# Where and when the first weights of an MLP are fetched and split, in a two-layer encoder

## The chip, the cores and the metric

The kernel runs on one core of one Trainium2 chip. The metric is the device time of one execution in microseconds (us), the median of several runs. The profile is a single execution taken by the hardware profiler.

## The reference

The program is a bidirectional encoder over 256 tokens with 1024 channels, of two layers, all in float32. Each layer has two sub-layers and each adds its result to the residual stream `h`:

```python
for layer in range(DEPTH):
    h = h + _token_mixer(_rmsnorm(h, norm1[layer]), ...)
    h = h + _conv_ffn(_rmsnorm(h, norm2[layer]), ...)
return _rmsnorm(h, norm_f)
```

The token mixer projects the normed tokens into a pooling branch, into queries, keys and values of 12 heads in three groups, and into two gates. Its end is what matters here:

```python
merged = jax.nn.sigmoid(g_pool) * (pool_out @ w_a) + jax.nn.sigmoid(g_attn) * (attn_out @ w_b)
return merged @ w_o
```

The MLP (`_conv_ffn`) multiplies the normed tokens by `w_up` (1024 x 5632), runs a width-3 convolution over tokens on the first half of the result, applies GELU, multiplies by the second half and then by `w_down` (2816 x 1024).

## The kernel before, in words

**Two-part numbers.** TensorE multiplies in a rounded float32 format. To keep float32 accuracy, each operand is split into a rounded high part and the low rest, and three products are summed: high x high, high x low and low x high. So every weight that arrives from memory is split before its use: ScalarE (ACT) casts the raw data to the high part (`wh`, line 197), and VectorE (DVE) subtracts it from the raw data to get the low part (`wl`, line 198).

**The stream of weights.** The class `Weights` holds one list of loads (1 MB each, 128 partitions x 2048 numbers, issued by SyncE, SP, at line 134) and one list of pieces, two for each load, in the order of use. A load goes to one of three rotating raw buffers (`RAW`), unless it has a `tag`: then it goes to the place of that name in a pool of large tiles, once the tile that had the place before is no longer read. A split piece goes to one of five rotating pairs `wh`, `wl` (`BUFS`), unless it has a `slot`: then it goes to a named large place as well. `get` hands out the next piece and has the pieces up to three further on split (`LOOK`); a piece with a slot may be split a little further ahead, since it takes none of the five pairs. Each split in turn asks for the loads up to two behind its own.

**Where an instruction stands in its queue.** Each engine works through its own queue in order. A scheduler puts the instructions there when the program is built. Two calls hold some of them back: `queue_behind(insts, n, first)` makes the splits of pieces `first` to `first + n - 1` stand behind the instructions `insts` in the queues of ACT and DVE, and `loads_behind` makes a load stand behind a given DMA in SP's queue.

**The stages around the change**, in each layer:
1. Scores of the attention heads. The last matmuls that read the keys of groups two and three (`kk`, place `k1`, line 998, named `k` in the trace) belong to the last head. They lie between the matmuls of `pool_out @ w_a`, which are line 643, as are all products that give rows of tokens.
2. The gates' stage: the pool gate in two halves of 512 channels (four loads of `w_in`), then for each half of the channels the attention gate (two loads of `w_in`) and `attn_out @ w_b` (one load).
3. The turn, once for each half: DVE multiplies gate and product (lines 1134, 1137), transposes 32 x 32 blocks (line 664), SP writes the result to memory (one DMA, `turned`, line 671) and reads it back by channels (four DMAs, `merged`, line 674), and ACT and DVE split it (lines 682, 683) into `m2`.
4. `residual_mm` with `w_o` (lines 561 to 563; eight pieces, of which the last four are held). The sum for the tokens is kept in four PSUM banks: token half 0 and 1, channels 0 to 511 and 512 to 1023. With the held pieces these are finished one after the other; the last one in two parts of 256 channels. As each is finished, `Norm.add` adds it to `h` on DVE (line 421) and sums its squares on ACT (line 423, `junk`). GpSimd (POOL) adds the two partial sums (line 432) and takes the power -1/2 (line 435). DVE scales four blocks of 256 channels (line 448, `xn`), PE transposes them to channels (line 457, `xt_ps`), and ACT and DVE split them (lines 460, 461) into `x2`, in the trace `x`.
5. The MLP's beginning (`begin_mlp`): the first 512 columns of `w_up`, in two loads, that is four pieces. The first three have slots: `v1` (the place of the values), `ybig` (of the product with `w_a`) and `at2` (of the attention's result); in the trace they are `v`, `ybig` and `at`. The fourth takes an ordinary pair `wh`, `wl`. PE's matmuls with these pieces are line 643 again, into `v_ps`.

The order of the four pieces and their loads is set at the end of the second turn (`n == 1`): the three loads from the MLP's first on stand behind the turn's last read (`there`), and the four pieces stand behind the split of that turn (`last`). The five pieces ahead of them, of `w_o`, stand behind the transposed blocks of the turn (`turned`).

Of the kernel before, what the change touches and what calls it, by code (L numbers as in the profile page):

```python
# [226 lines left out]
def encoder(ctx, tc, x, w_in, w_pool, pool_scale, w_a, w_b, w_o, norm1, norm2, w_up, conv_w,  # L227
# [11 lines left out]
    W = Weights(tc, wpool, big)  # L239

    def cols(w, c0):

        src = w[:, c0 : c0 + 256].rearrange("(k p) c -> p k c", p=P)
        return W.add(
            src, (8, 256), [((lambda t, j=j: t[:, :, j * P : (j + 1) * P]), (8, P)) for j in (0, 1)]
        )

    def rows(w, r0, n=2, c0=0, width=1024, tag=None, pieces=2):

        src = w[r0 : r0 + n * P, c0 : c0 + width].rearrange("(k p) c -> p k c", p=P)  # L250
        h = n // pieces
        return W.add(
            src, (n, width), [((lambda t, j=j: t[:, j * h : (j + 1) * h, :]), (h, width)) for j in range(pieces)],
            tag,
        )

    first_up = []
    for l in range(DEPTH):
        for g in range(NG):
            c0 = C_V + g * 512  # L260
            slots = (("m2", 0, 2), ("m2", 1, 2), ("ybig",), ("at2",)) if g == 0 else ()
            for j in range(2):
                tag = "k1" if l == 0 and g == 1 and j == 0 else None
                W.use(rows(w_in[l], j * 512, 4, c0, 512, tag), slots[2 * j : 2 * j + 2])
        if l == 0:
            W.n_scaled = len(W.pieces)
        for c in range(3, -1, -1):
            W.use(cols(w_in[l], c * 256))
        for n, c in enumerate(PAIRS):
            pool = ([], [])  # L270
            if n == 1:
                pool = W.add(
                    w_pool[l].rearrange("g (k p) c -> p (g k) c", p=P), (8, 256),
                    [((lambda t, j=j: t[:, 4 * j : 4 * j + 4, :]), (4, 256)) for j in range(2)],
                )
                pool = (pool[:1], pool[1:])
            W.use(pool[0] + cols(w_in[l], C_Q + c * 256))
            W.use(pool[1] + cols(w_in[l], C_K + c * 256))
        for w, c0 in ((w_a[l], 0), (w_in[l], C_GP)):
            for c in (c0, c0 + 512):  # L280
                W.use(rows(w, 0, 4, c, 512) + rows(w, 512, 4, c, 512))
        for c in (0, 512):
            W.use(rows(w_in[l], 0, 4, C_GA + c, 512) + rows(w_in[l], 512, 4, C_GA + c, 512))
            W.use(rows(w_b[l], 0, 4, c, 512))
        for c in range(4):
            W.use(rows(w_o[l], c * 256))
        first_up.append((len(W.pieces), len(W.loads)))
        slots = (("v1",), ("ybig",), ("at2",))
        for j in range(2):
            W.use(rows(w_up[l], j * 512, 4, 0, 512), slots[2 * j : 2 * j + 2])  # L290
        for f in range(0, NF, 2):
            a = cols(w_up[l], f * P) if f >= ENTRY else []
            g = cols(w_up[l], DFF + f * P)
            W.use([a[0], g[0], a[1], g[1]] if a else g)
            if f >= LAG:
                W.use(rows(w_down[l], (f - LAG) * P))
        for f in range(NF - LAG, NF, 2):
            W.use(rows(w_down[l], f * P))
# [349 lines left out]
    def by_tokens(x2, n, at_once=1, then=None):  # L648

        ps = [mmp.tile([P, 512], F32, tag="mm", name="t_ps") for _ in range(2)]  # L650
        for i0 in range(0, n, at_once):
            held = [W.get() for _ in range(at_once)]
            for t in range(2):
                for i, piece in enumerate(held, i0):
                    v_sum(ps[t], x2, t, i, piece, n - 1)
            for i, _ in held:
                W.free(i)
            if then:
                then()
        return ps  # L660

    def turn_blocks(y, t, rows):

        return nc.vector.transpose(out=y[:, :, :, t, :].rearrange("p q c j -> p c q j"), in_=rows)

    def to_chunks(y, z, x2):

        d = dram.tile([P, 4, 256], F32, tag="turned", bufs=2, name="turned")  # L670
        nc.sync.dma_start(out=d, in_=y.rearrange("p q c t j -> p q (c t j)"))
        for q in range(4):
            src = d[:, q].rearrange("(a i) x -> i a x", a=4)
            there = nc.sync.dma_start(
                out=z[32 * q : 32 * q + 32].rearrange("p a c t j -> p a (c t j)"), in_=src
            )
        for c in range(0, 4, 2):
            cs = slice(c, c + 2)
            src = z[:, :, cs].rearrange("p a c t j -> p a (c t) j")
            hi, lo = (p[:, cs].rearrange("p c t (a j) -> p a (c t) j", a=4) for p in x2)  # L680
            last = (
                nc.scalar.copy(out=hi, in_=src),
                nc.vector.tensor_sub(out=lo, in0=src, in1=hi.bitcast(F32)),
            )
        return there, last
# [179 lines left out]
    for l in range(DEPTH):  # L865
# [245 lines left out]
        def gate():  # L1111
            th = big.tile([P, 2, 512], F32, tag="gates", name="gates")
            ps = by_tokens(x2, 4)
            for t in range(2):
                nc.scalar.activation(th[:, t], ps[t], AF.Tanh, scale=0.5)
            return th
# [11 lines left out]
        for n, cc in enumerate(HALVES):  # L1128
            th = gate()
            ps = by_tokens(at2, 2, 2)  # L1130
            y = big.tile([P, 4, 4, 2, 32], F32, tag=("q0", "k0")[n], name="turned")
            for t in range(2):
                with tc.issue_after(last[1].ins) if n else ExitStack():
                    nc.vector.scalar_tensor_tensor(
                        out=th[:, t], in0=th[:, t], scalar=1.0, in1=ps[t], op0=ALU.add, op1=ALU.mult
                    )
                    nc.vector.tensor_add(out=th[:, t], in0=th[:, t], in1=pa[:, t, cc])
                    turned = turn_blocks(y, t, th[:, t])
                last = (None, turned)
            ks = slice(4 * n, 4 * n + 4)  # L1140
            there, last = to_chunks(y, z[:, n], (mh[:, ks], ml[:, ks]))

            piece, load = first_up[l]
            if n == 0:
                W.queue_behind((turned,), 1)
                W.loads_behind.update({load - 2: there, load - 1: there})
                W.queue_behind(last, 5, piece - 5)
            else:
                W.queue_behind((turned,), 5, piece - 5)
                W.loads_behind.update({load: there, load + 1: there, load + 2: there})  # L1150
                W.queue_behind(last, 4, piece)

        x2 = two_parts("x", "x2")
        norm = Norm(to_channels(x2, acc, g2))
# [28 lines left out]
        def keep_entry(ps):  # L1183
            r = sm.tile([P, ENTRY * P], F32, tag="p", bufs=3, name="a_rows")
            nc.scalar.copy(out=r, in_=ps)
            return r
# [17 lines left out]
        last = keep_entry(ps)  # L1204
# [99 lines left out]
```

## Time and profile before

| | us |
|---|---|
| median of three runs | 875.97 |
| lowest and highest run | 874.54, 877.9 |
| the profiled execution | 875.6 |
| its span, from the first to the last instruction | 873.8 |

How to read it: PE is TensorE's matmuls, DVE VectorE, ACT ScalarE, POOL GpSimd, SP SyncE, whose work here is to issue DMAs. A line of the timeline has the start and the duration in us, the engine, the line of the kernel, the operation, what it writes and reads, and the number of instructions put together; in brackets stands how long the engine was idle just before, and whose work ended that. Matmuls overlap: a row's duration is longer than the distance to the next row's start. A line of the waits has who waited for whom, the total in us, how often, and the longest. The mean granted clock of TensorE was 0.999 of full speed.

### The profile page before, as it was taken

Reading aid. Unit: us, or ns where it says so; the run is one execution under the profiler, and the core shown is the slowest. Engines: PE = TensorE matmul, PEld = TensorE weight load, DVE = VectorE, ACT = ScalarE, POOL = GpSimd, SP = SyncE. Lnnn points to the kernel's source line nnn. Section 1 sums busy time; section 2 is a strip of 40 time slices with the busy share of each in tenths; the row PEclk is TensorE's granted clock in tenths of the full one; section 3 lists DMA queues with packets and bytes.
Section 4 is the critical chain, followed back from the end, with each engine's and each line's share of the span. In section 5 each row is a group of like instructions: output and inputs, shape, how many; then the busy total and the mean of one; then the engine's idle time right before and its main releaser. Section 6 shows DMA issues by size and latency. Waiting matters only on the chain.

```text
span 873.8 us, 12139 instructions
## 1 busy us (share of the span) xinstructions
PE 864.0 (99%) x4583; PEld 744.5 (85%) x4583; DVE 662.2 (76%) x1070; ACT 510.2 (58%) x847; POOL 32.5 (4%) x98
## 2 busy tenths in 40 slices
PE   9999999999999999999999999999999999999997
PEld 8888888888878888888888889988888788888886
DVE  7998786656769978878855987765567798887884
ACT  7756554544457766666545674544444587666663
POOL 1800000000010000000000000000000100000000
PEclk9999999999999999999999999999999999999999
DMA  9676545445765465475636564453566446546531
GB/s 338 234 243 208 180 151 180 141 155 194 242 213 193 154 231 193 154 234 191 240 122 218 168 219 166 147 169 124 193 237 239 172 152 232 192 166 220 193 144 49
DMA packets 116547, 165.86 MB, mean 190 GB/s; under 512 B 3640, under 2 KB 84224, under 8 KB 116488
## 3 DMA queue, kind: packets, MB, share of 16 engines
q1 hardware_dynamic: 116328, 164.81, 55.8%
q8 instruction: 36, 0.59, 0.3%
q10 hardware_dynamic: 160, 0.27, 0.1%
q14 instruction: 23, 0.19, 0.1%
HBM read 161.90 MB, written 3.17 MB: 189 GB/s over the span
## 4 chain that ended last, share of the span: by engine, by line
PE 95%; DMA 2%; DVE 1%; ACT 1%; issue 0%; SPq 0%; POOL 0%; POOLq 0%; ACTq 0%; DVEq 0%
PE proj_ps L519 46%; PE t_ps L643 16%; PE v_ps L643 6%; PE res_ps L563 5%; PE res_ps L561 5%; PE res_ps L562 5%; PE v_ps L857 2%; PE v_ps L764 1%; PE pool_ps L519 1%; PE pt_ps L1027 1%; PE o_ps L1048 1%; PE s_ps L998 1%; DMA raw<-in_w_up_dram 1%; PE xt_ps L457 1%; PE s_ps L993 1%; PE o_ps L1044 1%
## 5 line engine op out<-in xcount | busy, mean ns | idle before, releaser
L198 DVE TENSOR_TENSOR wl<-raw,wh 128x1024 fp32r<-128x1024 f32 x274 | 333.5, 1222 | 140.2 <-ACT wh L197 99.2
L197 ACT CAST wh<-raw 128x1024 fp32r<-128x1024 f32 x274 | 286.3, 1049 | 137.1 <-PE t_ps L643 63.5
L519 PE MATMUL proj_ps<-x,wh 128*128 128x512 f32 x1152 | 274.6, 390 | 0.0
L519 PEld LDWEIGHTS proj_ps<-x,wh 128*128 128x128 f32 x1152 | 213.1, 188 | 42.2
L519 PEld LDWEIGHTS proj_ps<-x,wl 128*128 128x128 f32 x1152 | 144.9, 191 | 3.6
L519 PE MATMUL proj_ps<-x,wl 128*128 128x256 f32 x1152 | 147.9, 283 | 0.0
L643 PE MATMUL t_ps<-wh,x 128*128 128x512 f32 x256 | 79.7, 390 | 0.0
L561 PE MATMUL res_ps<-wh,actq 128*128 128x512 f32 (+1 forms) x184 | 70.0, 380 | 0.0
L562 PE MATMUL res_ps<-wl,actq 128*128 128x512 f32 (+1 forms) x184 | 69.9, 380 | 0.0
L563 PE MATMUL res_ps<-wh,actk 128*128 128x512 f32 (+1 forms) x184 | 69.9, 380 | 0.0
L643 PEld LDWEIGHTS t_ps<-wh,x 128*128 128x128 f32 x256 | 48.1, 188 | 9.9
L643 PE MATMUL t_ps<-wl,x 128*128 128x512 f32 x128 | 49.8, 389 | 0.0
L643 PE MATMUL t_ps<-wh,po 128*128 128x512 f32 x128 | 42.7, 399 | 0.0
L562 PEld LDWEIGHTS res_ps<-wl,actq 128*128 128x128 f32 x184 | 34.6, 188 | 6.6
L561 PEld LDWEIGHTS res_ps<-wh,actq 128*128 128x128 f32 x184 | 34.6, 188 | 6.6
L563 PEld LDWEIGHTS res_ps<-wh,actk 128*128 128x128 f32 x184 | 34.6, 188 | 6.6
L1230 ACT ACTIVATE y<-y 128x256 f32<-128x256 f32 x44 | 18.1, 417 | 28.5 <-DVE y L1221 28.4
L430 POOL TENSOR_SCALAR ss<-ss 128x1 f32<-128x1 f32 x8 | 2.4, 302 | 802.0 <-ACT junk L423 802.0
L1217 ACT ACTIVATE y<-a,prm 128x256 f32<-128x256 f32 x36 | 21.6, 600 | 14.8 <-DVE a L556 14.8
L643 PEld LDWEIGHTS t_ps<-wl,x 128*128 128x128 f32 x128 | 24.0, 188 | 5.0
L643 PEld LDWEIGHTS t_ps<-wh,po 128*128 128x128 f32 x128 | 24.1, 188 | 4.7
L563 PE MATMUL res_ps<-wh,m 128*128 128x512 f32 (+1 forms) x72 | 26.5, 369 | 0.0
(209 smaller groups left out, 1168.9 us busy)
## 6 DMA issues: line engine op xcount, KB each, us to landing
raw<-in_w_in_dram SPq DMA_DIRECT2D x58, 1024.0 KB, 5.6
raw<-in_w_up_dram SPq DMA_DIRECT2D x44, 1024.0 KB, 5.7
raw<-in_w_down_dram SPq DMA_DIRECT2D x22, 1024.0 KB, 4.7
raw<-in_w_a_dram SPq DMA_DIRECT2D x8, 1024.0 KB, 4.9
raw<-in_w_o_dram SPq DMA_DIRECT2D x8, 1024.0 KB
raw<-in_w_b_dram SPq DMA_DIRECT2D x4, 1024.0 KB
raw<-in_w_pool_dram SPq DMA_DIRECT2D x2, 1024.0 KB
turned<-turned SPq DMA_DIRECT2D x4, 512.0 KB
```

What stands on the lines that cost most here:

```text
L197: lambda: nc.scalar.copy(out=h, in_=src),
L198: lambda: nc.vector.tensor_sub(out=l, in0=src, in1=h.bitcast(F32)),
L457: nc.tensor.transpose(pt[:, k, :], xn[:, c0 : c0 + P], ident)
L519: nc.tensor.matmul(out, w(k), x, start=(steps is first and k == 0), stop=(steps is last and k == nk - 1), skip_group_check=turns["rest"],)
L561: nc.tensor.matmul(ps, ah, wh, start=first, stop=False, skip_group_check=on)
L562: nc.tensor.matmul(ps, ah, wl, start=False, stop=False, skip_group_check=on)
L563: nc.tensor.matmul(ps, al, wh, start=False, stop=last, skip_group_check=on)
L643: nc.tensor.matmul(ps, x2[:, 2 * n + j, part, t, :], w[:, j, :], start=(n + m == 0), stop=(n == last and m == 5),)
L764: return nc.tensor.matmul(ps[t], a[:, k, t, :], w[:, k % 2, :], start=first, stop=last)
L857: nc.tensor.matmul(ps[t], a[:, k, t, :], w[:, j, :], start=(k + m == 0), stop=(k == KD - 1 and m == 2),)
L1217: nc.scalar.activation(y, a, AF.Identity, bias=b, scale=w1)
L1230: nc.scalar.activation(y2, y, AF.Square, scale=float(np.sqrt(0.044715)))
```

## The change

The first load of the MLP's weights no longer takes a raw buffer. It goes to the place `k1` of the keys. It is taken out of the list of loads that stand behind the second turn's read, and the first of its two pieces is taken out of the pieces that stand behind the split of that turn. With nothing to hold it back, the load is issued when the keys are no longer read, and the piece is split as soon as `Weights` and the scheduler come to it, which is in the gates' stage. Its second piece, both pieces of the second load, and both later loads keep their places behind the turn. The computation is the same.

```diff
         slots = (("v1",), ("ybig",), ("at2",))
         for j in range(2):
-            W.use(rows(w_up[l], j * 512, 4, 0, 512), slots[2 * j : 2 * j + 2])
+            tag = None if j else "k1"
+            W.use(rows(w_up[l], j * 512, 4, 0, 512, tag), slots[2 * j : 2 * j + 2])
...
                 W.queue_behind((turned,), 5, piece - 5)
-                W.loads_behind.update({load: there, load + 1: there, load + 2: there})
-                W.queue_behind(last, 4, piece)
+                W.loads_behind.update({load + 1: there, load + 2: there})
+                W.queue_behind(last, 3, piece + 1)
```

## The prediction

> **What bounds the kernel now.** I read the page's busy times first, then what TensorE (PE) waited for, then the timeline of each engine around that wait.
>
> ```profile
> PE 864.0 (99%) x4583; PEld 744.5 (85%) x4583; DVE 662.2 (76%) x1070; ACT 510.2 (58%) x847; POOL 32.5 (4%) x98
> PE xt_ps L457 <- DVE xn L448: 3.3, 2, 1.7
> ```
>
> PE works for 864.0 of 873.8 us, so all its idle time is 9.8 us. In the list of waits (total, times, longest) it waits for another engine's result at one place only, once in each layer: the transposes `xt_ps` (L457) of the second norm, for `xn`, 3.3 us in all. Here is that place on PE in the first layer, and its twin in the second:
>
> ```profile
> 248.38 0.28 PE L563 MATMUL res_ps<-wh,m 128*128 128x256 f32 x1
> 250.32 0.83 PE L457 MATMUL xt_ps<-ident,xn 128*128 128x128 f32 x4 [1.66 <-DVE xn L448]
> ...
> 252.43 0.60 PE L457 MATMUL xt_ps<-ident,xn 128*128 128x128 f32 x4
> 252.78 1.78 PE L643 MATMUL v_ps<-v,x 128*128 128x512 f32 x6
> 254.40 1.53 PE L643 MATMUL v_ps<-ybig,x 128*128 128x512 f32 x6
> 255.76 1.53 PE L643 MATMUL v_ps<-at,x 128*128 128x512 f32 x6
> ...
> 681.24 0.83 PE L457 MATMUL xt_ps<-ident,xn 128*128 128x128 f32 x4 [1.65 <-DVE xn L448]
> ```
>
> The columns are start, duration, engine, line. PE ended L563 at 248.66 and stood 1.66 us. The group of four transposes then took 0.83 where the next took 0.60 (0.23 of restart). The first six matmuls of the MLP, on `v`, took 1.62 us to the start of the next six (252.78 to 254.40), those on `ybig` 1.36: 0.26 more, a small second wait. So this place costs 1.66 + 0.23 + 0.26 = 2.15 us a layer, 4.3 in two: **the most that the change can give here**, 0.49% of the time.
>
> What does `xn` wait for? The queues of ACT, DVE and POOL:
>
> ```profile
> 242.04 1.05 ACT L197 CAST v<-raw 128x1024 fp32r<-128x1024 f32 x1 [3.11 <-DMA raw<-in_w_up_dram]
> 243.00 1.05 ACT L197 CAST ybig<-raw 128x1024 fp32r<-128x1024 f32 x1
> 244.58 1.05 ACT L197 CAST at<-raw 128x1024 fp32r<-128x1024 f32 x1 [0.54 <-DMA raw<-in_w_up_dram]
> 247.85 0.63 ACT L423 ACTIVATE junk<-h 128x512 f32<-128x512 f32 x1
> 251.99 0.57 ACT L460 CAST x<-xt_ps 128x512 fp32r<-128x512 f32 x1
> ...
> 243.12 1.23 DVE L198 TENSOR_TENSOR v<-raw,v 128x1024 fp32r<-128x1024 f32 x1 [3.39 <-ACT v L197]
> 244.27 1.22 DVE L198 TENSOR_TENSOR ybig<-raw,ybig 128x1024 fp32r<-128x1024 f32 x1
> 245.40 0.68 DVE L421 TENSOR_TENSOR h<-res_ps,h 128x512 f32<-128x512 f32 x1
> 246.00 1.21 DVE L198 TENSOR_TENSOR at<-raw,at 128x1024 fp32r<-128x1024 f32 x1
> 247.14 0.68 DVE L421 TENSOR_TENSOR h<-res_ps,h 128x512 f32<-128x512 f32 x1
> 247.82 1.23 DVE L198 TENSOR_TENSOR wl<-raw,wh 128x1024 fp32r<-128x1024 f32 x1
> 249.78 0.88 DVE L448 SCALAR_TENSOR_TENSOR xn<-h,rstd,gain 128x256 f32<-128x256 f32 x2 [0.73 <-POOL rstd L435]
> 250.58 0.68 DVE L421 TENSOR_TENSOR h<-res_ps,h 128x512 f32<-128x512 f32 x1
> 252.63 0.68 DVE L461 TENSOR_TENSOR x<-xt_ps,x 128x512 fp32r<-128x512 f32 x1
> ...
> 248.72 0.38 POOL L432 TENSOR_TENSOR ss<-ss 128x1 f32<-128x1 f32 x1 [1.43 <-PE res_ps L563]
> ...
> 241.40 0.40 PE L563 MATMUL res_ps<-wh,m 128*128 128x512 f32 x1
> 244.12 0.39 PE L563 MATMUL res_ps<-wh,m 128*128 128x512 f32 x1
> ```
>
> `v` and `ybig` are the two pieces of the MLP's first load, `at` and the last `wh` those of its second. The first load landed at 242.0, and ACT starts its cast then, after 3.11 us idle. DVE then subtracts `v` (1.15 us to the next start) and `ybig`, and only then adds the residual's first half (L421, 245.40), though PE's last matmul for that half ended at 241.80; it subtracts `at`, and adds the second half at 247.14 to 247.82, which PE had finished by 244.51. The square on ACT (L423), two POOL steps and `xn` follow: from the end of that add to the start of the transposes, 250.32 − 247.82 = 2.50 us. The late load and three subtractions in DVE's queue hold PE.
>
> **The change part by part.** Comparing the two programs' instructions engine by engine: PE and POOL are the same; in each layer SP moves one load, ACT one cast, DVE one subtraction, and a few neighbours change places.
>
> *The load.* It is issued 21 DMAs earlier on SP, between the two loads of the pool gate's second half, and waits there only for PE's last read of the keys (L998); it is moved past eleven loads and the ten DMAs of the two turns.
>
> ```profile
> 157.94 0.61 PE L998 MATMUL s_ps<-k,q 128*128 128x128 f32 x4
> 155.55 0.37 SPq L134 DMA_DIRECT2D raw<-in_w_in_dram  x1
> 163.68 0.37 SPq L134 DMA_DIRECT2D raw<-in_w_in_dram  x1
> 173.62 0.37 ACT L1053 CAST at<-o_ps 128x256 fp32r<-128x256 f32 x1
> 176.43 1.05 ACT L197 CAST wh<-raw 128x1024 fp32r<-128x1024 f32 x1 [2.44 <-PE t_ps L643]
> 174.72 0.42 DVE L1054 TENSOR_TENSOR at<-o_ps,at 128x256 fp32r<-128x256 f32 x1
> 177.51 1.23 DVE L198 TENSOR_TENSOR wl<-raw,wh 128x1024 fp32r<-128x1024 f32 x1 [2.37 <-ACT wh L197]
> DMA to landing us min/median/max: 4.7/5.0/9.1
> 235.21 0.39 SPq L134 DMA_DIRECT2D raw<-in_w_up_dram  x1
> ```
>
> The keys are free at 158.55, after the load ahead was issued (155.55) and 5.1 us before the one behind it is (163.68, which waits for its own buffer). So SP is not held, and the 1 MB moves in a gap; even at the longest landing seen, 9.1 us (the line gives lowest, median, highest), it is there by 167.7, ahead of the cast below. Cost: nothing. Were the keys read later than 163.68, SP would hold back the next loads by the difference.
>
> *The split of `v`.* Its cast now stands behind the cast of `at` (173.62) and ahead of one at 176.43, which ACT reaches after idling 2.44 us for a buffer that PE frees; the cast takes 1.05. On DVE it stands between 174.72 and 177.51, in 2.37 us of idle time, and takes 1.22. Both gaps hold it. Cost: nothing; were they gone, 1.2 us on each engine, beside pieces that are split ahead of their use.
>
> *The second load* now stands first behind the turn's reads. Before, the first load was issued there at 235.21 and landed at 242.0, the second 0.5 later, landing in time for the cast at 244.58. The second now gets the earlier place, the same size and the same reads ahead of it, so I take 242.0. The bounds are the median landing, 235.21 + 5.0 = 240.2, and its old landing, 244.56; 242.0 is the row of the same place in the queue.
>
> *The order behind it.* ACT casts `ybig` before the landing, `at` at 242.04, then the last `wh`, and only then the squares. DVE: `ybig` (done before the landing), `at`, first add, last `wl`, second add. One subtraction fewer stands between landing and second add, but `wl` has moved ahead of it. By the spacings above: `at` 243.12, add 244.27, `wl` 244.87, add 246.01 to 246.69. That is 247.82 − 246.69 = **1.13 us earlier**. ACT is free by 244.1, so the square follows at once. Behind the second load the others come one buffer earlier, as many at a time as before; ACT splits them only from here on:
>
> ```profile
> 260.12 3.90 ACT L197 CAST wh<-raw 128x1024 fp32r<-128x1024 f32 x4
> ```
>
> PE waits for none of them before, so earlier is worth nothing there.
>
> *POOL.* Its sum took 0.38 us at 248.72, beside the subtraction of `wl` (247.82 to 249.05). The rows of the group (lowest, median, highest) and of the second layer:
>
> ```profile
> L432 POOL TENSOR_TENSOR ss<-ss x11: 192/193/432, 248.7 to 868.0; 128x1 f32<-128x1 f32 x11
> 679.58 0.43 POOL L432 TENSOR_TENSOR ss<-ss 128x1 f32<-128x1 f32 x1 [1.43 <-ACT junk L423]
> 680.70 0.88 DVE L448 SCALAR_TENSOR_TENSOR xn<-h,rstd,gain 128x256 f32<-128x256 f32 x2 [0.73 <-POOL rstd L435]
> 681.49 0.68 DVE L421 TENSOR_TENSOR h<-res_ps,h 128x512 f32<-128x512 f32 x1
> ```
>
> The median is 0.193, and 0.43 is the other slow one, again beside `wl`. Now `wl` is over by 246.1 and DVE stands idle: I count the median, 0.19 us saved in the first layer and 0.24 in the second. If the neighbour is not what slows the sum, the total below is 0.4 us less. The Trainium skill (SBUF — State Buffer, "Who interferes with whom") says that a VectorE instruction with two SBUF inputs, as this one has, shuts out a GpSimd instruction that reads SBUF; by that rule the 0.19 is right, and the trace agrees, the slow sum ending 0.05 us after the subtraction.
>
> *Given back.* `xn` starts at 249.78 − 1.13 − 0.19 = 248.46, and the transposes at 249.00: PE waits 0.34 us instead of 1.66. But a third `xn` block now goes ahead of the next add (L421, 250.58 before): it starts three blocks behind the first, 1.20 us instead of 0.80. The square behind that add, on ACT, stands ahead of the cast of `x` (251.99), and DVE's `x` (252.63) ends at 253.31, for which PE's matmuls on `v` wait already. So what counts there is 1.13 + 0.19 − 0.40 = **0.92 us**; the rest becomes a longer wait at those matmuls. From there PE is one unbroken chain, with all of the norm's second half shifted alike.
>
> *Sum.* First layer 0.92. Second layer the same with 0.24 for POOL: 0.97. Together 1.9 us: the profiled execution, 875.6 us with a span of 873.8, would take 873.7. It stands 0.4 under the median of 875.97, which becomes **874.1**.
>
> **The rivals.**
> *The second load lands late* (slower). If two queued loads share the engines and the place in the queue doesn't count, it lands as before, 244.56. Each step of the chain is then 2.54 us later than I set it: 2.54 − 0.92 = 1.6 us lost a layer, 3.2 in two, 879.2. It decides from a landing at 243.0, 0.92 after the one I take. For it: a load with 8x256 blocks is now behind the second one, which the trace doesn't show. Against it: the two landings before are 2.5 us apart. The Trainium skill (DMA: Bandwidth & Descriptors, "Queues, rings and completion order") says that each DMA engine consumes descriptors in ring order; by that this rival does not occur, and the two landings agree.
>
> *It lands early.* At 240.2 the chain gains 1.8 us more, and this place's waits go as far as they can: 4.3 us, 871.7. Against it: the turn's reads are still ahead, as they were for the 6.8 us from 235.21 to 242.0.
>
> *No gain.* The load and split move, but the second add does not come earlier: `wl`, two instructions with it, and the third `xn` eat it all, or a wait unseen at the last `wh` takes the place. 876.0. For it: 0.4 of 1.3 us is already lost to the reordering.
>
> **How the numbers follow.** Forecast 0.60, no gain 0.17, late landing 0.13, early 0.10. A landing 0.4 us off moves the forecast by 0.8; the runs shown reach from 1.4 below their median to 1.9 above. Its own range is 872.5 to 876.5; with the no-gain case, 872.2 to 877.0, leaving out most of the late and of the early case. About 0.5% (4.4 us) is what a measurement of this kernel can tell from no change. Even the early case is at its edge, and the late one inside: faster 0.05, same 0.91, slower 0.04.
>
> **What would show it.** Right: PE's waits at L457 sum to some 0.7 us instead of 3.3; the cast of `at` starts near 242.0, the first `xn` near 248.5; POOL's two slow sums near 0.19; the matmuls on `v` start 0.9 to 1.3 us earlier and stretch to about 2.0; nothing in the gates' stage moves. Wrong: a cast of `at` near 244.5, a wait of PE in the gates' stage, or L563 to L457 still 1.6 apart.

## The result and the profile after

| | before | changed |
|---|---|---|
| median (22 runs of each, same chip) | 875.98 us | 874.11 us |
| the profiled execution | 875.6 us | 874.23 us |
| its span | 873.8 us | 872.4 us |

The ratio of the times, changed to before, is 0.9977 with a 95% interval of 0.9969 to 0.9985: 0.23% faster. That is less than the half per cent which the prediction took as the least that a measurement of this kernel can tell, and it is clear of 1 all the same: the interval reaches 0.08% to each side. One run of the kernel before, of 1092.88 us, was a slow one and is left out of the ratio. The forecast was 874.1.

The page of the changed kernel, its span and its busy times; then the list of what PE waited for (total, times, longest):

```profile
span 872.4 us, 12133 instructions
PE 864.5 (99%) x4583; PEld 744.1 (85%) x4583; DVE 662.5 (76%) x1070; ACT 509.6 (58%) x847; POOL 31.8 (4%) x98
```

```profile
PE v_ps L765 <- DVE m L211: 0.8, 1, 0.8
PE gain_ps L349 <- PEq L1287: 0.8, 1, 0.8
PE res_ps L562 <- ACT m L683: 0.5, 1, 0.5
```

PE works as long as before. The wait for `xn` has left the list (3.3 us before; lines behind 290 stand one lower now, so L457 is L458). Two waits are new. (The one at `gain_ps`, ahead of all other work, is in the list of every kernel here.) That at L765 lies in the first microseconds, before anything that the change touches, and other executions of the same kernel show it or don't. That at L562 matters: PE waits for the split `m` of the second turn, the operand of the output projection. The timeline of PE at this place, in both layers:

```profile
228.29 0.39 PE L562 MATMUL res_ps<-wh,m 128*128 128x512 f32 x1
...
249.35 0.28 PE L564 MATMUL res_ps<-wh,m 128*128 128x256 f32 x1
249.47 0.60 PE L458 MATMUL xt_ps<-ident,xn 128*128 128x128 f32 x4
251.35 0.60 PE L458 MATMUL xt_ps<-ident,xn 128*128 128x128 f32 x4
251.74 1.92 PE L644 MATMUL v_ps<-v,x 128*128 128x512 f32 x6
253.50 1.53 PE L644 MATMUL v_ps<-ybig,x 128*128 128x512 f32 x6
...
682.20 1.92 PE L644 MATMUL v_ps<-v,x 128*128 128x512 f32 x6
683.96 1.54 PE L644 MATMUL v_ps<-ybig,x 128*128 128x512 f32 x6
```

From L564 to L458 PE goes through without a pause, and the transposes take 0.60, not 0.83. But L564 itself starts at 249.35, where it started at 248.38 before. What is left of the norm's wait now stands at the matmuls on `v`: 1.76 us to the next start (251.74 to 253.50), against 1.62 before and 1.48 where nothing waits (experiment 4).

To compare traces I use one distance, **D**: from PE's first matmul of the output projection (the first row above) to the start of the six matmuls on `ybig` (253.50). Behind it PE runs on unbroken. The same first row of the kernel before:

```profile
227.86 0.39 PE L561 MATMUL res_ps<-wh,m 128*128 128x512 f32 x1
```

D was 254.40 − 227.86 = 26.54 us in the first layer and is 253.50 − 228.29 = 25.21: 1.33 gained. In the second layer it was 26.46 and is 683.96 − 657.95 = 26.01: only 0.45. All else in the span agrees between the two traces: from the first layer's `ybig` matmuls to the second layer's projection 404.44 before and 404.45 now, and behind the last D 188.5 and 188.4. The first layer's projection starts 0.43 later here. That is none of the change's doing: it is there in the first microseconds, when PE waits 0.84 for a result of DVE that waits for a first load (its first matmul into `v_ps` started at 5.37 before), and it is still 0.43 at the last matmuls that read the keys, which started at 157.94 before:

```profile
5.87 0.47 PE L765 MATMUL v_ps<-m,xuh 128*128 128x512 f32 x1 [0.84 <-DVE m L211]
...
158.37 0.61 PE L999 MATMUL s_ps<-k,q 128*128 128x128 f32 x4
```

From there to the projection PE takes 69.92 us in both layers now, and took 69.92 and 69.91 before. So the gates' stage is as long as it was, in both layers.

The queues that decide D; ACT with the cast of the turn's result (`m`) and the cast `at` of the second load, in both layers, then DVE and POOL:

```profile
238.79 1.14 ACT L683 CAST m<-merged 128x512 fp32r<-128x512 f32 x2 [1.09 <-DMA merged<-turned]
242.09 1.05 ACT L197 CAST at<-raw 128x1024 fp32r<-128x1024 f32 x1 [1.21 <-DMA raw<-in_w_up_dram]
...
668.78 1.14 ACT L683 CAST m<-merged 128x512 fp32r<-128x512 f32 x2 [1.42 <-DMA merged<-turned]
672.54 1.05 ACT L197 CAST at<-raw 128x1024 fp32r<-128x1024 f32 x1 [1.68 <-DMA raw<-in_w_up_dram]
```

```profile
243.18 1.23 DVE L198 TENSOR_TENSOR at<-raw,at 128x1024 fp32r<-128x1024 f32 x1 [1.03 <-ACT at L197]
244.32 0.68 DVE L422 TENSOR_TENSOR h<-res_ps,h 128x512 f32<-128x512 f32 x1
244.92 1.22 DVE L198 TENSOR_TENSOR wl<-raw,wh 128x1024 fp32r<-128x1024 f32 x1
246.05 0.68 DVE L422 TENSOR_TENSOR h<-res_ps,h 128x512 f32<-128x512 f32 x1
248.51 1.28 DVE L449 SCALAR_TENSOR_TENSOR xn<-h,rstd,gain 128x256 f32<-128x256 f32 x3 [1.78 <-POOL rstd L436]
249.71 0.69 DVE L422 TENSOR_TENSOR h<-res_ps,h 128x512 f32<-128x512 f32 x1
251.72 0.69 DVE L462 TENSOR_TENSOR x<-xt_ps,x 128x512 fp32r<-128x512 f32 x1 [0.26 <-ACT x L461]
...
247.64 0.19 POOL L433 TENSOR_TENSOR ss<-ss 128x1 f32<-128x1 f32 x1 [1.42 <-ACT junk L424]
678.08 0.19 POOL L433 TENSOR_TENSOR ss<-ss 128x1 f32<-128x1 f32 x1 [1.42 <-ACT junk L424]
```

`at` landed at 242.09, the second add starts at 246.05, `xn` at 248.51 in three blocks, POOL's sums take 0.19. The chain came as it was forecast, to within 0.1 us at each of these.

In the gates' stage the moved load and split stand where they were expected: SP, ACT and DVE:

```profile
159.01 0.37 SPq L134 DMA_DIRECT2D raw<-in_w_up_dram  x1
...
174.32 1.05 ACT L197 CAST v<-raw 128x1024 fp32r<-128x1024 f32 x1
...
176.86 1.05 ACT L197 CAST wh<-raw 128x1024 fp32r<-128x1024 f32 x1 [1.49 <-PE t_ps L644]
...
175.49 1.22 DVE L198 TENSOR_TENSOR v<-raw,v 128x1024 fp32r<-128x1024 f32 x1
177.94 1.23 DVE L198 TENSOR_TENSOR wl<-raw,wh 128x1024 fp32r<-128x1024 f32 x1 [1.24 <-ACT wh L197]
```

ACT's idle time ahead of the cast of `wh` shrinks from 2.44 to 1.49 and still ends with PE: the cast of `v` lies inside it.

### The profile page after: what moved, and what is told of

The parts are those of the page before. It is cut to its first block, busy times and chain, and to the rows that moved or that the text cites. A ratio compares the mean times of both kernels' runs of the same rounds, so it can differ in the third digit from the quotient of the medians.

```text
span 872.4 us, 12133 instructions
## 1 busy us (share of the span) xinstructions
PE 864.5 (99%) x4583; PEld 744.1 (85%) x4583; DVE 662.5 (76%) x1070; ACT 509.6 (58%) x847; POOL 31.8 (4%) x98
## 4 chain that ended last, share of the span: by engine, by line
PE 92%; DMA 4%; DVE 2%; SPq 1%; ACT 1%; issue 1%; POOLq 0%; ACTq 0%; POOL 0%; DVEq 0%
PE proj_ps L520 46%; PE t_ps L644 14%; PE v_ps L644 6%; PE res_ps L562 5%; PE res_ps L564 5%; PE res_ps L563 5%; PE v_ps L858 3%; DMA merged<-turned 2%; PE v_ps L765 1%; PE pool_ps L520 1%; DMA turned<-turned 1%; PE pt_ps L1028 1%; PE o_ps L1049 1%; PE s_ps L999 1%; PE s_ps L994 1%; PE o_ps L1045 1%
## 5 line engine op out<-in xcount | busy, mean ns | idle before, releaser
L562 PE MATMUL res_ps<-wh,actq 128*128 128x512 f32 (+1 forms) x184 | 69.9, 380 | 0.0
L564 PE MATMUL res_ps<-wh,actk 128*128 128x512 f32 (+1 forms) x184 | 69.9, 380 | 0.0
L562 PEld LDWEIGHTS res_ps<-wh,actq 128*128 128x128 f32 x184 | 34.6, 188 | 6.6
L564 PEld LDWEIGHTS res_ps<-wh,actk 128*128 128x128 f32 x184 | 34.6, 188 | 6.6
L1218 ACT ACTIVATE y<-a,prm 128x256 f32<-128x256 f32 x36 | 21.6, 600 | 14.7 <-DVE a L557 14.7
L562 PE MATMUL res_ps<-wh,m 128*128 128x512 f32 (+1 forms) x72 | 26.7, 371 | 0.6 <-ACT m L683 0.5
```

The source lines that it names most:

```text
L562: nc.tensor.matmul(ps, ah, wh, start=first, stop=False, skip_group_check=on)
L564: nc.tensor.matmul(ps, al, wh, start=False, stop=last, skip_group_check=on)
L1218: nc.scalar.activation(y, a, AF.Identity, bias=b, scale=w1)
```

## The experiments

My theory: the landing of the load that is first in the queue behind the turn sets DVE's order, and with it PE. The change puts the second load there, which needs one subtraction fewer ahead of the second add. Rivals: it is the place of the split that counts (two instructions less in a crowded queue), or the large place itself, in which a load waits for no raw buffer. All edits below are shown against the changed kernel. Where they add or drop lines, the line numbers in the traces shift by up to three.

**1. The load moved, the split not.** The load is issued early as in the change; both its pieces are split behind the turn as before.

```diff
-                W.queue_behind(last, 3, piece + 1)
+                W.queue_behind(last, 4, piece)
```

> The change with the first load early, in the keys' place, but its first piece split behind the second turn again, as before the change. My theory (the second load's landing and the subtractions behind it hold PE): the first two pieces are split between the turn's split and that landing, where DVE stood idle 3.4 us; the second add comes where it does in the change, and the time is that of the change, 874.1 us, 1.9 under before. The rival (the split taken out of that stage is what gains): about 876.

Measured: 873.94 against 876.38 for the kernel before, ratio 0.9966 (0.9953 to 0.998), span 871.5. It gains no less than the change, so the place of the split isn't what brings the gain. (The kernel before was raised here by runs at a lower granted clock; more of that under 2.) In the second layer `at` lands 14.25 us after the projection starts and D is 25.67, a difference of 11.42, the changed kernel's. In the first layer the load was there before ACT came to it: `at` was cast at 241.06, 12.91 after the projection's start, right behind `ybig`. There the split behind the turn does cost something, as DVE's rows show:

```profile
240.24 1.23 DVE L198 TENSOR_TENSOR v<-raw,v 128x1024 fp32r<-128x1024 f32 x1 [0.18 <-ACT v L197]
241.38 1.22 DVE L198 TENSOR_TENSOR ybig<-raw,ybig 128x1024 fp32r<-128x1024 f32 x1
242.51 1.22 DVE L198 TENSOR_TENSOR at<-raw,at 128x1024 fp32r<-128x1024 f32 x1
```

Three subtractions in a row: `at` starts 1.45 us after its cast instead of 1.09. Splitting `v` in the gates' stage saves that 0.36 where the second load lands early; where it lands near 14, nothing.

**2. The place moved, the load not.** The first load gets the keys' place and is issued behind the turn as before, with both splits there.

```diff
-                W.loads_behind.update({load + 1: there, load + 2: there})
-                W.queue_behind(last, 3, piece + 1)
+                W.loads_behind.update({load: there, load + 1: there, load + 2: there})
+                W.queue_behind(last, 4, piece)
```

> The first load goes to the keys' place, but it is issued behind the turn's read and its piece split behind the turn, as before. My theory: the second load lands second again, near 244.5 on the scale of before, the queues of DVE and ACT are those of before, PE waits 1.6 us at the second norm in each layer: 876.0. The rival (the raw buffer set free, with the later loads earlier, is what gains): 874.1.

Measured: 874.93 against 876.38, ratio 0.9996 (0.9979 to 1.0012): by the ratio no gain, as the theory has it, though this interval and the change's overlap by a little and the medians lie 1.45 apart. Most of that goes with TensorE's granted clock: 11 of the 23 runs of the kernel before on this chip and 3 of the 12 of this version show 0.995 to 0.997 and took 876.1 to 880.3 us. The other runs, at 0.998 or more, have medians of 874.81 and 874.57; the runs of experiment 1, all at 0.998 or 0.999, 873.94. The trace separates the versions better. The queues of ACT, DVE and POOL are in the order of before, POOL's sum is slow again, and in this execution the first load landed early. ACT and POOL, first layer:

```profile
241.33 1.05 ACT L197 CAST v<-raw 128x1024 fp32r<-128x1024 f32 x1 [1.97 <-DMA raw<-in_w_up_dram]
243.89 1.06 ACT L197 CAST at<-raw 128x1024 fp32r<-128x1024 f32 x1 [0.56 <-DMA raw<-in_w_up_dram]
...
248.02 0.37 POOL L433 TENSOR_TENSOR ss<-ss 128x1 f32<-128x1 f32 x1 [1.43 <-ACT junk L424]
```

D is 25.42 here, near the changed kernel's, only because the load landed at 13.07 and not 14.18. From landing to `ybig` matmuls it is 12.35, as before. Its second layer landed early too (12.98), so the D of this one execution says little about the version's time; the constant of 12.35 behind the landing does.

**3. Both kernels again**, one more execution each on that chip, for the spread of the landings.

> The kernel before, once more, for a second profile: how far the landing of the turn's reads and of the loads behind them differ from one execution to the next. If the 0.6 and 1.0 us by which the turn's second reads landed later in the changed kernel are chance, they differ by as much here; if the change causes them, they stand again at 3 us from issue and PE waits 0.1 us for that split.

> The changed kernel, once more, for a second profile. If the late landing of the turn's second reads belongs to the change, PE waits again 0.5 to 1.0 us for their split in both layers; if it is chance, the waits differ from those of the first profile, and the sum of what PE waits at the norm and in the MLP's first matmuls stays as it was: none to 0.4 at the transposes, 0.4 at the matmuls.

Measured: before 875.32 (span 873.5), changed 873.67 (span 871.9). The waits of PE at this place, first in the kernel before, then in the changed one; then the changed one's casts of `at` in both layers, and SP's issues of the loads there (the first of the two counts):

```profile
PE xt_ps L457 <- DVE xn L448: 2.0, 2, 1.7
PE res_ps L561 <- ACT m L682: 0.3, 1, 0.3
```

```profile
PE xt_ps L458 <- DVE xn L449: 0.9, 1, 0.9
```

```profile
242.60 1.06 ACT L197 CAST at<-raw 128x1024 fp32r<-128x1024 f32 x1 [2.63 <-DMA raw<-in_w_up_dram]
...
671.64 1.06 ACT L197 CAST at<-raw 128x1024 fp32r<-128x1024 f32 x1 [0.54 <-DMA raw<-in_w_up_dram]
...
235.34 0.94 SPq L134 DMA_DIRECT2D raw<-in_w_up_dram  x2
...
666.37 0.94 SPq L134 DMA_DIRECT2D raw<-in_w_up_dram  x2
```

The same load, at the same place behind the same reads, took 7.26 us from issue to cast in one layer and 5.27 in the other. The wait moves with it: 0.9 in the first layer, none in the second.

The late `m` of the first profile is not shown to be the change's doing: the kernel before has it here too, with a wait of 0.3 for it. In the table below `m` starts at 10.19 on the mean in six layers with the order of before (experiment 2 among them) and at 10.41 in six of the changed kernel, each from 9.9 to 10.8; so small a difference is not told from chance here.

**4. Both loads early.** The second load gets a large place as well (`xn`'s), so no split behind the turn waits for a load.

```diff
-            tag = None if j else "k1"
-            W.use(rows(w_up[l], j * 512, 4, 0, 512, tag), slots[2 * j : 2 * j + 2])
+            W.use(rows(w_up[l], j * 512, 4, 0, 512, ("k1", "xn")[j]), slots[2 * j : 2 * j + 2])
...
-                W.loads_behind.update({load + 1: there, load + 2: there})
+                W.loads_behind.update({load + 2: there})
```

> The change, and also the second load early, in a second place that is dead from the scores on (that of the low parts of queries and keys). No load that the norm's queue needs is late then; the last three pieces are split from 238.9 on the scale of before, and the second add comes when PE has finished it, at 244.6. My theory: PE waits neither at the transposes nor at the MLP's first matmuls, and the whole 2.15 us a layer goes: 871.7, 2.4 under the change. The rival (the landing is not what binds, the turn's reads or something behind them is): 874.1 as the change.

Measured: 872.48 against 875.36, ratio 0.9972 (0.996 to 0.9983), span 870.3. PE's wait at this place, and its matmuls in the first layer:

```profile
PE res_ps L561 <- ACT m L682: 0.2, 1, 0.2
```

```profile
228.08 0.39 PE L561 MATMUL res_ps<-wh,m 128*128 128x512 f32 x1
...
250.89 1.64 PE L643 MATMUL v_ps<-v,x 128*128 128x512 f32 x6
252.37 1.54 PE L643 MATMUL v_ps<-ybig,x 128*128 128x512 f32 x6
```

No wait for `xn`, nor at `v` (1.48 to the next start). D is 252.37 − 228.08 = 24.29, PE without a pause. By the medians 2.9 us are gained where 4.3 were expected. In the second layer D is 24.94: the turn's result `m` came 0.64 later there (10.56 after the projection's start against 9.92), and D is longer by as much. The list has only 0.2 of it, because the matmuls that follow start 0.33 to 0.39 apart, not 0.23 as elsewhere in this projection.

**5. The fourth piece behind the second add.** The changed kernel, with the split of the last `wh`, `wl` held until DVE's add of the second half (the add is kept by `Norm.add`):

```diff
...
+            W.queue_behind((norm.adds[0, 1],), 1, first_up[l][0] + 3)
             ps, held = v_tile(), [W.get() for _ in range(4)]
```

> The change, with the split of the fourth piece held behind the second add. One subtraction fewer stands between the second landing and that add. My theory: the add comes 1.1 us earlier than in the change, PE does not wait at the transposes, some 0.3 us stays at the matmuls, and POOL's sum is slow again where it lies beside that subtraction: 872.3. The rival (only the landing counts, not the queue behind it): 874.1.

Measured: 872.77 against 875.36, ratio 0.9973 (0.9963 to 0.9984), span 871.1. DVE and POOL:

```profile
245.72 0.69 DVE L422 TENSOR_TENSOR h<-res_ps,h 128x512 f32<-128x512 f32 x1 [1.28 <-PE res_ps L565]
246.33 1.22 DVE L198 TENSOR_TENSOR wl<-raw,wh 128x1024 fp32r<-128x1024 f32 x1
...
247.32 0.28 POOL L434 TENSOR_TENSOR ss<-ss 128x1 f32<-128x1 f32 x1 [1.81 <-ACT junk L425]
```

DVE now idles 1.28 us ahead of the second add until PE has the sum: DVE no longer sets the time. And `wl` is beside POOL's sum again: the sum takes 0.28 and ends at 247.60, 0.05 after the subtraction (247.55).

**6. The third `xn` block behind the add.** The changed kernel, with the later blocks of the first token half held until the next half's first add, to get back what the forecast called given back (the adds are kept as in 5):

```diff
...
+                held = norm.adds[1, 0] if psum is acc and t == 0 and n > 1 else None
+                with tc.issue_after(held.ins) if held else ExitStack():
...
```

> The change, with the third and fourth block of xn of the first half of the tokens held behind the third add. My theory (the third block ahead of that add gives 0.40 us a layer back): DVE's subtraction for x ends 0.4 us earlier, PE's wait at the MLP's first matmuls falls from 0.4 to 0.0 or 0.1 us, and the time is 873.3. The rival (the two orders come to the same): 874.1, with the wait as it was.

Measured: 873.09 against 875.36, ratio 0.9979 (0.9967 to 0.999), span 870.6. DVE:

```profile
248.09 0.88 DVE L452 SCALAR_TENSOR_TENSOR xn<-h,rstd,gain 128x256 f32<-128x256 f32 x2 [1.78 <-POOL rstd L437]
248.88 0.68 DVE L422 TENSOR_TENSOR h<-res_ps,h 128x512 f32<-128x512 f32 x1
...
250.94 0.68 DVE L465 TENSOR_TENSOR x<-xt_ps,x 128x512 fp32r<-128x512 f32 x1
```

From the first `xn` to the end of DVE's `x`: 251.62 − 248.09 = 3.53 us, which was 3.53 before and is 252.41 − 248.51 = 3.90 in the changed kernel. So 0.37 is what the block's new place costs. It is paid only where the landing sets D, and in this execution it didn't.

**7. Three versions on one chip**: 5 and 6 together, the changed kernel, and 4 again.

> The change, with both orders set by hand: the fourth piece's split behind the second add, and the third and fourth block of xn behind the third add; the second load stays late. My theory: behind a landing at time T after PE's first matmul of the output projection, the six matmuls on ybig start at T + 10.0 us, against T + 11.4 in the change and T + 12.4 before; with landings of 12.8 to 14.7 seen, PE waits for nothing there in most layers, and the stage is 24.3 us plus what PE waits for the turn's split. Time some 1.5 under the change: 872.6. The rival (the order on DVE is without effect beside the landing): 874.1.

> The changed kernel, timed on the same chip as the two versions beside it. My theory: 1.9 us under the kernel before, and 1.5 to 2 over the two versions; the six matmuls on ybig start 11.4 us behind the landing, or as early as PE gets there, 24.3. The rival (the versions come to the same): all three within 0.5 us.

> The version with both loads early, once more, beside the changed kernel. My theory: in each layer the six matmuls on ybig start 24.3 us behind PE's first matmul of the output projection, plus what PE waits for the turn's split, whatever the loads do; 1.5 to 2 us under the changed kernel. The rival (it comes to the same as the change): within 0.5 us.

Measured against 875.03: 5 and 6 together 872.43, ratio 0.9974 (0.9966 to 0.9983); the changed kernel 873.36, 0.998 (0.9968 to 0.9992); 4 again 872.44, 0.9965 (0.9947 to 0.9982). Both versions have medians 0.9 us below the changed kernel, less than expected. The intervals against the kernel before overlap, but the runs themselves lie apart: 9 of 12 and 5 of 6 are below 872.7 us, and of the changed kernel's 11 one is. The profiled execution of 5 and 6 together (span 874.1) reached the first projection 2 us late, at 230.35; it was as late at the last matmuls that read the keys (160.43), so this comes from ahead of the place and doesn't touch D. PE's wait at this place, in both layers:

```profile
PE res_ps L565 <- ACT m L686: 1.3, 2, 0.8
```

Nothing waits for `xn` any more; the turn's result, `m`, is all that is left at this place.

**All traces together.** Times in us from the projection's first matmul, first layer / second layer: `m`, the start of the cast of the turn's result; T, the start of the cast of the load first in the queue (`v` before, `at` in the changed kernel), which waits for that load everywhere but in 1, first layer; and D.

| kernel | m | T | D | D − T | D − m |
|---|---|---|---|---|---|
| before | 9.93 / 9.91 | 14.18 / 14.06 | 26.54 / 26.46 | **12.36 / 12.40** | 16.61 / 16.55 |
| before again | 10.17 / 10.71 | 14.37 / 13.53 | 26.71 / 25.95 | **12.34 / 12.42** | 16.54 / 15.24 |
| 2, place alone | 9.96 / 10.47 | 13.07 / 12.98 | 25.42 / 25.39 | **12.35 / 12.41** | 15.46 / 14.92 |
| changed | 10.50 / 10.83 | 13.80 / 14.59 | 25.21 / 26.01 | **11.41 / 11.42** | 14.71 / 15.18 |
| changed again | 9.95 / 10.51 | 14.68 / 13.14 | 26.08 / 24.91 | **11.40** / 11.77 | 16.13 / **14.40** |
| changed, third | 10.45 / 10.21 | 12.91 / 14.29 | 24.83 / 25.73 | 11.92 / **11.44** | **14.38** / 15.52 |
| 1, load alone | 9.96 / 9.76 | 12.91 / 14.25 | 24.67 / 25.67 | 11.76 / **11.42** | 14.71 / 15.91 |
| 6, `xn` held | 10.44 / 10.06 | 12.97 / 13.01 | 24.83 / 24.44 | 11.86 / 11.43 | **14.39 / 14.38** |
| 5, fourth held | 10.77 / 10.42 | 13.30 / 12.80 | 25.14 / 24.81 | 11.84 / 12.01 | **14.37 / 14.39** |
| 5 and 6 | 11.14 / 10.88 | 14.07 / 13.73 | 25.52 / 25.28 | 11.45 / 11.55 | **14.38 / 14.40** |
| 4, both early | 9.92 / 10.56 | none waits | 24.29 / 24.94 | | **14.37 / 14.38** |
| 4 again | 10.12 / 10.43 | none waits | 24.51 / 24.82 | | **14.39 / 14.39** |

Two differences are constant where they apply (bold). D is the later of two ends: m + 14.38, the output projection on PE without a pause once the turn's result is there; and T + 12.38 in the order of before, or T + 11.42 in that of the change. In the order of before, the load's end was later in all six layers shown. In the changed kernel it was later in four of six; in two the turn's result was. One layer (1, first) fits neither, by the 0.36 found there. In 5, 6 and both together the turn's result was the later end in all six layers, and would have been with a constant of 11.42 too. So their D does not measure how much earlier their orders end behind the landing (T + 10.0 was expected of both together); that part of the expectation stays open.

## Why the prediction was right, step by step

*What bounds the kernel.* Right: PE, and this place. The ceiling of 2.15 us a layer is borne out: 26.42 (the mean D of four layers before) less 24.29 (experiment 4, first layer, PE without a pause) is 2.13. Of its parts the 0.26 at the matmuls on `v` was too much: they take 1.48 to the next start where nothing waits, so 0.14 of the 1.62 was a wait. Experiment 4 got 1.78 a layer (the mean D of its four layers is 24.64), not 2.15, because what the prediction did not name stood behind: the read-back of the second turn. `m` starts between 9.8 and 11.1 in all kernels, and each tenth beyond 9.9 is PE's once the load's end no longer covers it.

*The moved load and the split of `v` cost nothing.* Right: the gates' stage takes the same time in both layers (69.92), and ACT's idle time covers the cast.

*The landing at 242.0.* Right on the mean: T averages 14.04 in four layers before and 13.90 in six of the changed kernel, so the second load does take the first's place. That the value came so close (242.09) is luck: the projection began 0.43 later in this execution, so behind its first matmul the landing was at 13.80 and not at 14.18, and in the second layer it was at 14.59. The mean stands for a spread of 12.9 to 14.7 that I had not seen in the two layers of one trace. The early-landing rival thus happens in part of the layers, and the wait for `m` takes part of what it would bring. The late rival needs T past 15.14 (243.0 − 227.86); no layer came there. I didn't try a forced late landing with the order unchanged.

*The order behind it, 1.13 us earlier.* Right: from the cast of the first landed piece to the second add 5.10 us before (247.14 − 242.04), now 246.05 − 242.09 = 3.96. That is 1.14.

*POOL, 0.19 and 0.24.* Right: both sums take 0.19. Experiment 2, which has the order of before, has 0.37 again, and 5, which puts `wl` back beside the sum, 0.28. By the rule of the Trainium skill (SBUF — State Buffer, "Who interferes with whom") a VectorE instruction with two SBUF inputs contends with a GpSimd instruction that reads SBUF; the trace agrees, the sum ending 0.05 us after the subtraction in 5 as in the kernel before.

*Given back, 0.40.* Measured 0.37 (experiment 6).

*Net 0.92 and 0.97, together 1.9.* Right for the order: at equal landing it is 12.38 − 11.42 = 0.96 a layer. The "no gain" rival is out: a constant of 12.38 would have stayed, as it did in experiment 2. The medians differ by 1.87 and on the third chip by 1.67.

That the median met the forecast so closely is partly luck, for two things that the sum does not have pull against each other. First, an early landing gains less than 0.96, because the turn's result binds then. The mean D is 25.46 in six layers of the changed kernel. In the kernel before it is 26.42, which is 0.96 more, but its four layers landed late; with experiment 2, which has the same order and landed early (13.0), it is 26.08 in six layers, 0.62 more, or 1.2 us for both layers. Second, the times of the order of before contain runs at a lower clock: of all executions whose granted clock is on record, 21 of 83 in that order show 0.995 to 0.997, and 1 of 92 in all the other orders. On the third chip the runs at 0.998 or more have medians of 874.40 before and 873.36 changed, 1.04 apart and not 1.67 (the means 1.42). So at equal clock the change is worth rather 1.0 to 1.4 us than 1.9. How much of the 1.87 goes with the clock can't be said: for those runs of the kernel before it is not on record.

The profiled execution itself gained 1.4: D fell by 1.33 and by 0.45, together 1.78, and 0.43 of that was lost in the first microseconds, ahead of anything that the change moves.

*The signs.* The matmuls on `v` start 1.04 us earlier and last 1.92, as given (0.9 to 1.3, about 2.0). One sign did not come: PE's wait at the transposes was to be 0.7 in all and is not in the list. PE itself came there 0.97 later in the first layer (249.35 against 248.38), 0.43 by its later start and the rest by the wait for `m`, for which the prediction had no term.

What failed in the follow-up: I expected more of 4, and of 5 with 6, than they gave: they are 0.9 us better than the changed kernel by their medians. They removed the wait for the load; the turn's result then stood behind it.

## What to carry to other kernels

When a wait follows from where a transfer stands in the queue, write its end as "landing plus a constant" for each order of the instructions, and compare the constants: they held to 0.1 us here, where the landings spread by 1.8 us. Before counting a wait's whole length as a gain, look for the next event at the same place that it covers; here it was the turn's result, up to 1.2 us later than in the layer where PE went on without a pause (11.14 against 9.92). Two executions of each kernel show how far a landing in a single trace may be trusted. And put the granted clock beside each time before you compare medians: here it made up part of a difference that looked like the forecast.

## What was not expected of the hardware

A 1 MB load at one place of the queue took from 5.2 to 7.3 us from issue to the start of the cast that waits for it, in executions of one kernel (changed kernel, third execution: issued at 235.86, cast at 241.07; changed again: the 7.26 above). The order of the issues ahead of it was the same. The load was issued 7.36 to 7.87 us after the projection's first matmul in the six layers of the changed kernel, and the two issued last (7.70 and 7.87) were cast first (12.91 and 13.14); but in 5 loads issued at 7.36 and 7.42 were cast at 12.80 and 13.30, so the issue doesn't explain it. What sets it, and the 1.4 us by which the start of `m` spreads, was not found; it stays open.

Runs at a granted clock of 0.995 to 0.997, which took 875.9 to 880.3 us, are almost all of the order in which PE stands longest at this place (21 of 83 executions, against 1 of 92 in the other orders, that one at 875.01). Whether that wait lowers the clock is not shown: no such run was profiled.
